# A hybrid S5 and linear-attention layer on one core: operand copies staged through tiles, 16 more weight tiles in the last sweeps, fewer and re-queued conditioning steps

## The chip, the cores and the metric

The kernel runs on one core of a Trainium2 chip, in one launch. The metric is the device time of that launch in microseconds. Before the change three runs took 2925.06, 2934.24 and 2933.97 us, median 2933.97. The names of the engines are those of the profile: PE is TensorE (PEld its weight loads), DVE is VectorE, ACT is ScalarE, POOL is GpSimd and SP is SyncE. SP and POOL issue nearly all transfers, each in the order of its own queue; ACT issues a few.

## The reference

One layer of a decoder. 1088 tokens (64 of the samples, 1024 of the prompt) of width 2048 are normed and modulated by a conditioning vector, then multiplied by one wide matrix whose columns feed two mixers and their gates:

```python
mod = jax.nn.silu(c) @ w_ada + b_ada
shift, scale, gate = jnp.split(mod, 3, axis=-1)
h = rms_norm(x, norm_gain) * (1 + scale[:, None]) + shift[:, None]
u_a, z_a, q, k, v, z_b, g_lr, m_a, m_b = jnp.split(h @ w_in, SPLIT_POINTS, axis=-1)
a_y, sa_re, sa_im = s5_branch(u_a, ...)
a_out = (a_y * jax.nn.silu(z_a)) @ w_a_out
log_a = jax.nn.log_sigmoid((g_lr @ w_gate_up + b_gate).astype(jnp.float32)) / GATE_TAU
b_y, s_gla = gla_branch(q * DK_B ** -0.5, k, v, log_a, s0_gla, gla_norm_gain)
b_out = (b_y.astype(x.dtype) * jax.nn.silu(z_b)) @ w_b_out
merged = jax.nn.sigmoid(m_a) * a_out + jax.nn.sigmoid(m_b) * b_out
y = x + gate[:, None] * (merged @ w_out)
```

All of it is float32. The S5 mixer is a diagonal complex scan in 64 groups; the other mixer is gated linear attention (GLA) with 4 heads. A final norm follows.

## The kernel before

Every wide product is made of three passes: an operand is split into a rounded part (`hi`) and the rest (`lo`), and PE adds hi·hi, hi·lo and lo·hi (`mm3`, lines 71 to 73; in the sweeps lines 1176 to 1178). Weights come in tiles of 128x512 floats (256 KB): SP loads one into a raw tile, ACT makes its `whi`, DVE its `wlo`.

The program has these stages, with their times in the profiled execution:

- 0 to 180 us: `norm_in` loads x and norms it. Then the columns 0 to 2 of `w_in` (the generator `product_k`) are multiplied while the conditioning product runs: 64 loads of 512 KB of `w_ada` (tile `adaraw`, line 195) and 512 small matmuls (`ada_mm`, line 203); each two chunks of it let `modulate` write two of the 16 operands `h[k]` (tiles `hh` and `hl`, lines 266 and 268).
- 180 to 664 us: further columns of `w_in`, with the S5 scan of 16 units woven in.
- 664 to 774 us: columns 20 to 23. Beside them `blocks` writes the right operands of the sweeps to DRAM: the splits of four sums `t1` to `t4` per k through the tile `st` (3 buffers; ACT line 1074, DVE line 1075, POOL's store line 1076, destination `opt`), and three plain quarters `11`, `21`, `22` per k straight from `hh` and `hl` (POOL lines 1079 and 1080, destination `op`, 48 stores in all).
- 774 to 1998 us: the `sweeps`. 48 columns are done by a Winograd scheme of seven half-size products: three groups of eight column pairs, seven sweeps each (`a11`, `a12`, `s1`, `s2`, `s3`, `a22`, `s4`), 384 matmuls of 272 columns a sweep. For each pair `left` loads weights into `raws()` (8 half act tiles and 2 `wraw` tiles, ten in turn); `s1`, `s2`, `s3` and `s4` load two tiles for one and subtract or add them on DVE (line 1109), `s1` and `s2` also store the result to `ws` (lines 1119 and 1122). After a pair, `right` loads the next sweep's operand (line 1142), and the results go to `mas`, `mbs`, `zas`, `zbs` through `fin` or `pt` (line 1196). The GLA mixer (`gla_run`) is woven in: `next(self.steps)` is called at the places in a pair that `self.pace[r]` gives, up to three.
- 1998 to 2500 us: `branch_a` (tile `yt`: 64 loads of 68 KB of the S5 result, line 993, then gelu) and `merge`, which multiplies by `w_a_out` and `w_b_out` in turn, loads `m` (line 1041) for each and stores `mscr`. The conditioning of the output gate (`ada_gates`: 32 loads `gateraw` of 512 KB, line 965, two buffers, and 256 small matmuls) is woven in, one step at the end of each of the three chunks of a product.
- 2500 us to the end: `final`, the product with `w_out` and the last norm.

What stands in the file isn't the order of the queues. Instructions are recorded with the tiles that they read and write, and a scheduler of the language then places them, engine by engine, by its own estimate of when each can start; an instruction recorded late stands early in its queue when its operands and its tiles are there early. A tile with few buffers holds its writers back until a buffer comes free, and a pool opened in the memory of a closed one waits for that one's last reader. Each engine then runs its queue strictly in order. So the 48 stores of lines 1079 and 1080, which need no tile of their own, stand at the head of POOL's queue, and the `yt` loads stand in the third group of the sweeps, when the GLA mixer's memory has come free for them.

Of the kernel before, what the change touches and what calls it, by code (L numbers as in the profile page):

```python
# [10 lines left out]
F32 = mybir.dt.float32  # L11
F32R = mybir.dt.float32r
U8 = mybir.dt.uint8
AF = mybir.ActivationFunctionType
# [4 lines left out]
P = 128  # L19
# [5 lines left out]
T = TS + TP  # L25
CH = [(0, 320), (320, 384), (704, 384)]
HT = T // 2
# [3 lines left out]
QK4 = 512  # L31


class Hybrid:
# [923 lines left out]
    def ada_gates(self):  # L958

        nc, a = self.nc, self.a  # L960
        for j in range(16, 24):
            ps = self.psum(False)
            for k in range(0, KT, 4):
                raw = self.p2.tile([P, 1024], F32, tag="raw", name="gateraw", bufs=2)
                nc.sync.dma_start(raw, a["w_ada"][j][:, k * 256:(k + 4) * 256])
                yield
                self.ada_mm(ps, k, raw, 4)
            yield
            self.ada_out(j, ps)
# [59 lines left out]
    def merge(self, aa):  # L1029

        nc, a = self.nc, self.a
# [3 lines left out]
        def gated(m, keep):  # L1035
# [14 lines left out]
            return ev  # L1050
        ea, eb = gated(self.mas, True), gated(self.mbs, False)
        self.product(a["w_a_out"], range(0, 3), aa, ea)
        bb = [self.branch_b(i) for i in range(8)]
        self.product(a["w_b_out"], range(0, 3), bb, eb)
        for j in range(3, 16):
            self.product(a["w_a_out"], [j], aa, ea)
            self.product(a["w_b_out"], [j], bb, eb)

# [6 lines left out]
    def blocks(self, h):  # L1065

        nc = self.nc
        V = nc.vector
        with ExitStack() as ctx:
            pp = self.pool("blocks", ctx=ctx)  # L1070
# [6 lines left out]
            for k in range(8):  # L1077
                for name, (hi, lo), o in (("11", h[8 + k], 0), ("21", h[k], 0), ("22", h[k], HT)):
                    nc.gpsimd.dma_start(self.opscr[name][k][:, :HT], hi[:, o:o + HT].bitcast(F32))
                    nc.gpsimd.dma_start(self.opscr[name][k][:, HT:], lo[:, o:o + HT].bitcast(F32))  # L1080
                x, y = (pp.tile([P, T], F32, tag=n, name=n, bufs=2) for n in "xy")
# [51 lines left out]
    def sweeps(self, w, groups, h):  # L1133

        nc = self.nc
# [12 lines left out]
        count = [0, 0]  # L1148

        def raws():  # L1150
            i = count[0] % 10
            count[0] += 1
            if i > 7:
                return self.wp.tile([P, QK4], F32, tag="wraw", name="wraw", bufs=2)
            return rawv[i]

        def fin():
            count[1] += 1
            return finv[count[1] % 8]
        n = 0  # L1160
        for g, group in enumerate(groups):
            for r, (an, bn) in enumerate(self.SWEEPS):
                B, N = sets[n % 2], sets[(n + 1) % 2]
                n += 1
                nxt = self.SWEEPS[r + 1][1] if r < 6 else "11" if g + 1 < len(groups) else None
                for i, (pair, dst, silu) in enumerate(group):
                    ps = self.pmm.tile([P, 2, 512], F32, tag="mm2", name="mm", bufs=2)
                    for q in range(2):
                        hi, lo = self.left(w, an, pair, q, self.wscr[i], raws)
                        for k in range(4):  # L1170
                            c = slice(k * P, (k + 1) * P)
                            bhi, blo = B[4 * q + k]
                            for m in range(2):
                                o = ps[:, m, :NC]
# [3 lines left out]
                                nc.tensor.matmul(o, lo[:, c], bh, start=False, stop=q == 1 and k == 3)  # L1178
                            if 4 * q + k in ((), (4,), (2, 6), (1, 4, 6))[self.pace[r]]:
                                next(self.steps, None)  # L1180
# [117 lines left out]
    def run(self):  # L1298
        nc, a = self.nc, self.a
# [59 lines left out]
        self.steps = self.behind()  # L1359
        self.pace = (3, 2, 2, 2, 1, 3, 2)  # L1360
        pairs = lambda j0, d, silu=False: [((j0 + i, j0 + i + 1), (d[i], d[i + 1]), silu) for i in range(0, len(d), 2)]
# [8 lines left out]
        self.steps = self.ada_gates()  # L1370
        self.ticks = ()
        self.merge(aa)
# [79 lines left out]
```

## Time and profile before

| what | value |
|---|---|
| median of three runs | 2933.97 us |
| the profiled execution, its span | 2938.97 us, 2937.2 us |
| PE busy, PEld busy | 96%, 91% |
| DVE, ACT, POOL busy | 58%, 35%, 14% |
| mean granted TensorE clock | 0.982 |
| moved by DMA | 610.52 MB, 208 GB/s over the span |

The page says that PE is the engine that everything waits for. It is read by stretches: in each, the time that PE is not busy, and the time that it runs at half its clock, are what could be saved there; the DMA share (the mean busy share of the 16 DMA engines) and the rows of waits say what it was for. Matmul ends are modelled, so a busy stretch can still hold small waits.

### The profile page before, as it was taken

How to read it: one execution, taken by the hardware profiler on the slowest of the kernel's cores; microseconds unless marked ns; L12 is line 12 of the kernel's file. 1: busy time of each engine (PE TensorE's matmuls, PEld its weight loads, DVE VectorE, ACT ScalarE, POOL GpSimd, SP SyncE). 2: the span in 40 equal slices, each digit the busy share in tenths (PEclk: the TensorE clock that was granted, in tenths of full speed). 3: DMA queues.
4: the chain of work that ended last, by engine and by line, in shares of the span. 5: the costliest groups of instructions: out<-in, count | busy, mean ns of one | idle time of the engine just before them, and what ended most of it. 6: DMA issues, size and time to landing. Idle time of an engine off the chain costs nothing.

```text
span 2937.2 us, 54282 instructions
## 1 busy us (share of the span) xinstructions
PE 2813.0 (96%) x20736; PEld 2669.6 (91%) x20736; DVE 1715.7 (58%) x4016; ACT 1018.9 (35%) x1823; POOL 411.5 (14%) x702
## 2 busy tenths in 40 slices
PE   7999999999899999999999989999999999899987
PEld 4689899999888999998999989999988999899987
DVE  3486777678245786667777535656532322456465
ACT  4222222223233344444344442333221211344434
POOL 1101222121001100011000032011110000203021
PEclk9999999999899999999999999999999999999999
DMA  9944444447668887668867599953575433555455
GB/s 377 386 132 133 117 127 122 114 122 258 235 206 288 295 298 255 187 217 302 292 219 246 194 276 296 319 181 123 173 257 176 136 120 118 184 161 181 145 181 164
DMA packets 321748, 610.52 MB, mean 208 GB/s; under 512 B 47952, under 2 KB 106096, under 8 KB 321360
## 3 DMA queue, kind: packets, MB, share of 16 engines
q1 hardware_dynamic: 256624, 433.51, 46.4%
q0 software_dynamic: 48528, 158.70, 15.6%
q10 hardware_dynamic: 16336, 14.84, 1.5%
q8 instruction: 163, 2.67, 0.4%
q14 instruction: 97, 0.79, 0.1%
HBM read 465.65 MB, written 132.87 MB: 204 GB/s over the span
## 4 chain that ended last, share of the span: by engine, by line
PE 63%; DMA 18%; DVE 8%; issue 7%; ACT 3%; POOL 1%; SPq 1%; DVEq 0%; POOLq 0%; ACTq 0%
PE mm L71 12%; PE mm L72 12%; PE mm L73 12%; PE mm L1178 6%; PE mm L1177 6%; PE mm L1176 6%; DMA raw<-in_w_in_dram 5%; DMA wraw<-in_w_in_dram 2%; DMA hh<-opt 1%; DMA bz<-zbs 1%; DMA raw<-ws 1%; DMA wraw<-in_w_out_dram 1%; PE bg L203 1%; DVE wlo L58 1%; DVE wlo L1130 1%
## 5 line engine op out<-in xcount | busy, mean ns | idle before, releaser
L1176 PE MATMUL mm<-hh,whi 128*128 128x272 f32 x2688 | 788.9, 293 | 25.4 <-ACT whi L1128 13.1
L1178 PE MATMUL mm<-hh,wlo 128*128 128x272 f32 x2688 | 790.2, 294 | 1.6 <-DVE wlo L1130 1.6
L1177 PE MATMUL mm<-hl,whi 128*128 128x272 f32 x2688 | 785.6, 292 | 0.0
L71 PE MATMUL mm<-ahi,whi 128*128 128x384 f32 (+3 forms) x1656 | 547.6, 331 | 17.9 <-DVE y L1248 9.0
L73 PE MATMUL mm<-ahi,wlo 128*128 128x384 f32 (+3 forms) x1656 | 544.2, 329 | 0.6 <-DVE wlo L58 0.4
L72 PE MATMUL mm<-alo,whi 128*128 128x384 f32 (+3 forms) x1656 | 543.5, 328 | 0.0
L1176 PEld LDWEIGHTS mm<-hh,whi 128*128 128x128 f32 x2688 | 514.3, 191 | 31.3 <-ACT whi L1128 14.7
L1178 PEld LDWEIGHTS mm<-hh,wlo 128*128 128x128 f32 x2688 | 513.8, 191 | 5.2 <-DVE wlo L1130 2.4
L1177 PEld LDWEIGHTS mm<-hl,whi 128*128 128x128 f32 x2688 | 514.3, 191 | 3.1 <-issue 1.0
L58 DVE TENSOR_TENSOR wlo<-wraw,whi 128x512 fp32r<-128x512 f32 x368 | 269.5, 740 | 269.8 <-ACT whi L56 268.4
L56 ACT ACTIVATE whi<-wraw 128x512 fp32r<-128x512 f32 x368 | 230.3, 630 | 490.5 <-PE mm L72 278.4
L71 PE MATMUL mm<-hh,whi 128*128 128x384 f32 (+3 forms) x1056 | 344.2, 329 | 9.0 <-ACT hh L266 9.0
L72 PE MATMUL mm<-hl,whi 128*128 128x384 f32 (+3 forms) x1056 | 346.8, 329 | 2.8 <-DVE hl L268 2.8
L73 PE MATMUL mm<-hh,wlo 128*128 128x384 f32 (+2 forms) x1056 | 346.6, 330 | 0.0
L71 PEld LDWEIGHTS mm<-ahi,whi 128*128 128x128 f32 x1656 | 314.6, 190 | 35.2 <-issue 22.8
L73 PEld LDWEIGHTS mm<-ahi,wlo 128*128 128x128 f32 x1656 | 314.5, 190 | 3.9 <-DVE wlo L58 2.5
L72 PEld LDWEIGHTS mm<-alo,whi 128*128 128x128 f32 x1656 | 315.0, 190 | 1.3 <-issue 0.4
L1128 ACT ACTIVATE whi<-raw 128x512 fp32r<-128x512 f32 x270 | 168.6, 628 | 323.3 <-PE mm L1177 191.6
L1130 DVE TENSOR_TENSOR wlo<-raw,whi 128x512 fp32r<-128x512 f32 x270 | 183.9, 684 | 51.4 <-ACT whi L1128 48.6
L71 PEld LDWEIGHTS mm<-hh,whi 128*128 128x128 f32 x1056 | 198.4, 189 | 14.2 <-ACT hh L266 11.5
L72 PEld LDWEIGHTS mm<-hl,whi 128*128 128x128 f32 x1056 | 198.9, 189 | 9.9 <-DVE hl L268 4.7
L73 PEld LDWEIGHTS mm<-hh,wlo 128*128 128x128 f32 x1056 | 198.8, 189 | 3.4 <-issue 2.6
(373 smaller groups left out, 3446.1 us busy)
## 6 DMA issues: line engine op xcount, KB each, us to landing
raw<-in_w_in_dram SPq DMA_DIRECT2D x346, 256.0 KB
wraw<-in_w_out_dram SPq DMA_DIRECT2D x192, 256.0 KB
wraw<-in_w_in_dram SPq DMA_DIRECT2D x182, 256.0 KB
adaraw<-in_w_ada_dram SPq DMA_DIRECT2D x64, 512.0 KB
hl<-opt SPq DMA_DIRECT2D x96, 272.0 KB
hh<-opt SPq DMA_DIRECT2D x96, 272.0 KB
raw<-ws SPq DMA_DIRECT2D x78, 256.0 KB
ws<-raw POOLq DMA_DIRECT2D x77, 256.0 KB, 5.5
```

The source lines that it names most:

```text
L56: nc.scalar.activation(hi, raw, AF.Copy)
L58: nc.vector.tensor_tensor(lo, raw, hi.bitcast(F32), ALU.subtract)
L71: nc.tensor.matmul(ps, hi[:, c], ah[:, sl], start=start, stop=False)
L72: nc.tensor.matmul(ps, hi[:, c], al[:, sl], start=False, stop=False)
L73: nc.tensor.matmul(ps, lo[:, c], ah[:, sl], start=False, stop=stop)
L203: self.nc.tensor.matmul(ps[i:i + 32, :256], self.c32[:, k, :], raw[:, (k - k0) * 256:(k - k0 + 1) * 256], start=k < 4, stop=k >= KT - 4, t ...
L1128: nc.scalar.activation(hi, x, AF.Copy)
L1130: nc.vector.tensor_tensor(lo, x, hi.bitcast(F32), ALU.subtract)
L1176: nc.tensor.matmul(o, hi[:, c], bh, start=q + k == 0, stop=False)
L1177: nc.tensor.matmul(o, hi[:, c], bl, start=False, stop=False)
L1178: nc.tensor.matmul(o, lo[:, c], bh, start=False, stop=q == 1 and k == 3)
```

## The change

Five things are changed.

- `blocks`: the quarters `11`, `21` and `22` are copied by ACT into the same `st` tile (two copies of 128x544 each), and one store of 544 KB takes the place of two of 272 KB. 24 stores and 48 ACT copies stand for 48 stores.
- `pace`: a table for each group in place of one for all; none in the third.
- From the third sweep (`s1`) of the last group to the end of its sixth, the steps of GLA are drained, and a pool `more` in its memory gives 16 further raw tiles, taken in turn with the old ten.
- `ada_gates` loads on POOL's queue in place of SP's.
- In `merge`, from column 3 on, only the products with `w_b_out` call its steps.

```diff
@@ ada_gates
-                nc.sync.dma_start(raw, a["w_ada"][j][:, k * 256:(k + 4) * 256])
+                nc.gpsimd.dma_start(raw, a["w_ada"][j][:, k * 256:(k + 4) * 256])
@@ merge
+        self.ticks = ()
         self.product(a["w_a_out"], range(0, 3), aa, ea)
...
+        gates = self.steps
         for j in range(3, 16):
+            self.steps = iter(())
             self.product(a["w_a_out"], [j], aa, ea)
+            self.steps = gates
             self.product(a["w_b_out"], [j], bb, eb)
@@ blocks
-                for name, (hi, lo), o in (("11", h[8 + k], 0), ("21", h[k], 0), ("22", h[k], HT)):
-                    nc.gpsimd.dma_start(self.opscr[name][k][:, :HT], hi[:, o:o + HT].bitcast(F32))
-                    nc.gpsimd.dma_start(self.opscr[name][k][:, HT:], lo[:, o:o + HT].bitcast(F32))
+                for name, hl, o in (("11", h[8 + k], 0), ("21", h[k], 0), ("22", h[k], HT)):
+                    st = pp.tile([P, T], F32R, tag="st", name="st", bufs=3)
+                    for p in range(2):
+                        nc.scalar.activation(st[:, p * HT:(p + 1) * HT], hl[p][:, o:o + HT].bitcast(F32), AF.Copy)
+                    nc.gpsimd.dma_start(self.opscr[name][k], st.bitcast(F32))
@@ sweeps
         def raws():
-            i = count[0] % 10
             count[0] += 1
+            if sp and count[0] % 2:
+                return sp.tile([P, QK4], F32, tag="raw2", name="raw2", bufs=16)
+            i = (count[0] // 2 if sp else count[0]) % 10
...
+            last = g + 1 == len(groups)
+            pace = ((2, 2, 2, 2, 2, 3, 2), (3, 3, 2, 2, 2, 3, 2), (0,) * 7)[g]
...
+                if last and r == 2:
+                    for _ in self.steps:
+                        pass
+                    sctx = ExitStack()
+                    sp = self.pool("more", ctx=sctx)
+                elif last and r == 6:
+                    sp = None
+                    sctx.close()
...
-                            if 4 * q + k in ((), (4,), (2, 6), (1, 4, 6))[self.pace[r]]:
+                            if 4 * q + k in ((), (4,), (2, 6), (1, 4, 6))[pace[r]]:
@@ run
-        self.pace = (3, 2, 2, 2, 1, 3, 2)
...
-        self.ticks = ()
```

What it moves is seen in the queues. First POOL's queue from its last setting-up instruction on, before (the first of 48 stores; `op_0_254` and the like are DRAM operands, the numbers being those of the tensors):

```order
masks.py:199 AFFINE_SELECT ident<-ident 128x128
L1079 DMA op_0_254<-hh 128x544
L1079 DMA op_1_255<-hh 128x544
L1080 DMA op_0_254<-hl 128x544
L1079 DMA op_0_214<-hh 128x544
L1080 DMA op_1_255<-hl 128x544
L1079 DMA op_1_215<-hh 128x544
```

and the same place now, where the S5 parameters follow at once:

```order
masks.py:199 AFFINE_SELECT ident<-ident 128x128
L415 DMA s5par<-par 128x2368
L421 DMA par<-s5par 128x148
L423 DMA bc<-in_s5bc_dram 128x256
L421 DMA par<-s5par 128x148
```

All 48 stores have left this place. They are now 24 in the stretch of columns 20 to 23, three ahead of each k's four. Its end on POOL's queue, before (`xr` is a tile of the program's last stage whose first three loads stand here; it shares its buffers with `ev`, from which the columns 22 and 23 are stored to `kscr`):

```order
L1076 DMA opt_7_229<-st 128x1088
L1076 DMA opt_7_245<-st 128x1088
L1076 DMA opt_7_237<-st 128x1088
L1076 DMA opt_7_253<-st 128x1088
L1237 DMA xr<-in_xT_dram 128x416 x3
L948 TENSOR_TENSOR on<-on 128x64
```

and now (line 1086 is the new store, line 1080 the old store 1076, line 1257 the old 1237):

```order
L1086 DMA op_7_213<-st 128x1088
L1086 DMA op_7_221<-st 128x1088
L1086 DMA op_7_261<-st 128x1088
L1257 DMA xr<-in_xT_dram 128x416 x3
L1080 DMA opt_7_229<-st 128x1088
L1080 DMA opt_7_245<-st 128x1088
L1080 DMA opt_7_237<-st 128x1088
L1080 DMA opt_7_253<-st 128x1088
L948 TENSOR_TENSOR on<-on 128x64
```

The last four stores now stand behind the three `xr` loads. On PE the first instruction of GLA (line 777) stood before the first matmul of the sweeps:

```order
L71 MATMUL bg<-hh,whi 128x384
L72 MATMUL bg<-hl,whi 128x384
L73 MATMUL bg<-hh,wlo 128x384
L777 MATMUL bg<-gr,wgu 128x64
L1176 MATMUL mm<-hh,whi 128x272
```

and it stands now behind 215 of them:

```order
L1197 MATMUL mm<-hl,whi 128x272
L777 MATMUL bg<-gr,wgu 128x64
L803 MATMUL bg<-q,k 32x32 x2
L1198 MATMUL mm<-hh,wlo 128x272
L1196 MATMUL mm<-hh,whi 128x272
```

The 20 units of GLA end accordingly 0.67 sweeps later, in the middle of the last group's second sweep. Third, POOL's queue at the start of the last group, before (`zas` is a result of the sweeps, `ws` the stored sum of two weight tiles):

```order
L993 DMA yt<-y_106 16x8x136 x4
L993 DMA yt<-y_107 16x8x136 x4
L1196 DMA zas_122<-fin 128x544
L1196 DMA zas_124<-fin 128x544
L993 DMA yt<-y_108 16x8x136 x4
L993 DMA yt<-y_109 16x8x136 x4
L1119 DMA ws_0_262<-raw 128x512
```

and now (lines 1216 and 1125 are the old 1196 and 1119):

```order
L948 TENSOR_TENSOR on<-on 128x256
L1216 DMA zas_126<-fin 128x544
L1216 DMA zas_128<-fin 128x544
L1216 DMA zbs_130<-fin 128x544
L1125 DMA ws_0_262<-raw_20930 128x512
L1125 DMA ws_0_262<-raw_20963 128x512
L1125 DMA ws_0_264<-raw_21000 128x512
L1216 DMA zbs_132<-fin 128x544
```

The `yt` loads are gone from here; they stand in the last group's sixth and seventh sweep. The `gateraw` loads stand on POOL's queue behind the sweeps, between the loads of `m` and the stores of `mscr`, the last behind 2112 of the 5184 matmuls of that part on PE, where it was 1536.

## Rows read from the trace of the kernel before

**Rows 1.** The page: busy time and share of the span by engine.

```profile
PE 2813.0 (96%) x20736; PEld 2669.6 (91%) x20736; DVE 1715.7 (58%) x4016; ACT 1018.9 (35%) x1823; POOL 411.5 (14%) x702
```

**Rows 2.** Stretches: length, busy time of PE, PEld, DVE, ACT, POOL, clock, DMA share, GB/s.

```profile
50.00:150.00 100.00, 91.43 (x684) 64.92 (x681) 41.72 (x105) 20.68 (x31) 20.87 (x39) 0.93 0.99 385
150.00:180.00 30.00, 25.07 (x180) 20.20 (x179) 22.05 (x75) 7.78 (x11) 4.29 (x8) 1.00 0.56 162
...
664.00:748.00 84.00, 84.00 (x507) 84.00 (x506) 70.03 (x94) 32.09 (x54) 16.74 (x32) 1.00 0.74 271
...
774.00:856.00 82.00, 70.10 (x475) 62.72 (x474) 29.82 (x91) 31.20 (x68) 1.95 (x4) 0.83 0.54 168
856.00:1623.00 767.00, 747.48 (x7087) 715.87 (x7086) 533.73 (x1295) 332.39 (x667) 80.58 (x144) 0.99 0.79 262
...
1681.00:1850.00 169.00, 151.73 (x1154) 150.00 (x1153) 79.06 (x123) 56.24 (x70) 47.24 (x88) 0.95 0.93 289
1850.00:1998.00 148.00, 144.27 (x1150) 143.51 (x1149) 96.09 (x143) 58.33 (x79) 21.53 (x39) 1.00 0.71 236
...
2100.00:2300.00 200.00, 194.20 (x1261) 171.31 (x1260) 71.11 (x112) 45.36 (x59) 18.45 (x35) 0.98 0.65 219
```

**Rows 3.** Waits of PE, 34 to 180 us: total, times, longest.

```profile
PE mm L71 <- ACT hh L266: 9.0, 6, 2.7
...
PE bg L203 <- DMA adaraw<-in_w_ada_dram: 1.1, 2, 0.6
```

**Rows 4.** DMA issues: times, KB each, median us to landing.

```profile
opt<-st POOLq DMA_DIRECT2D x32, 544.0 KB, 4.5
...
op<-hl POOLq DMA_DIRECT2D x24, 272.0 KB, 8.9
```

**Rows 5.** Timeline of POOL, lines 1079, 1076, 1237: start, duration, operation, idle before.

```profile
49.27 0.71 POOL L1079 DMA_DIRECT2D op<-hh  x1 [47.96 <-ACT hh L266]
...
673.43 1.11 POOL L1076 DMA_DIRECT2D opt<-st  x2 [28.39 <-DVE st L1075]
...
747.78 0.53 POOL L1076 DMA_DIRECT2D opt<-st  x1 [1.90 <-DVE st L1075]
784.23 0.55 POOL L1237 DMA_DIRECT2D xr<-in_xT_dram  x1 [35.92 <-DMA kscr<-ev]
```

**Rows 6.** The chain that ended last, 0 to 200 us: start, duration.

```profile
94.41 1.98 PE bg L203 x32
```

**Rows 7.** Groups of 664 to 748 us: busy, mean ns, idle before.

```profile
L1076 POOL DMA_DIRECT2D opt<-st x32 | 17.1, 533 | 86.2 <-DVE st L1075 82.6 <-issue 3.7
L1074 ACT ACTIVATE st<-x 128x544 fp32r<-128x544 f32 x24 | 15.7, 658 | 19.1 <-DMA opt<-st 13.6 <-DVE x L1091 3.6 <-DVE y L1084 1.3
```

**Rows 8.** Timeline of ACT: the last thing ahead of GLA's first matmul.

```profile
759.61 0.24 ACT L776 ACTIVATE gr<-gt 96x64 fp32r<-96x64 f32 x1
```

**Rows 9.** Waits of PE and of ACT at the first sweep.

```profile
PE bg L833 <- DVE g L820: 4.9, 2, 4.4
...
ACT ev L637 <- DMA kscr<-ev: 4.8, 3, 3.0
```

**Rows 10.** Waits of PE and DVE, 1681 to 1850 us.

```profile
PE mm L1176 <- ACT whi L1128: 10.5, 2, 5.5
...
DVE raw L1109 <- DMA raw<-in_w_in_dram: 38.4, 12, 8.5
```

**Rows 11.** Loads of `yt`, 1640 to 1860 us, and two stretches of 10 us.

```profile
L993 POOL DMA_DIRECT2D yt<-y x48: 528/530/559, 1683.3 to 1786.4; - x48
...
1700.00:1710.00 10.00, 10.00 (x82) 10.00 (x81) 1.85 (x3) 6.08 (x6) 1.10 (x2) 1.00 0.90 215
1850.00:1860.00 10.00, 10.00 (x83) 10.00 (x82) 4.95 (x8) 3.18 (x4) 0.00 (x0) 1.00 1.04 378
```

**Rows 12.** Waits of SP's queue and of PE, 2095 to 2300 us.

```profile
SPq L965 <- PE bg L203: 119.6, 28, 17.6
...
PE bg L203 <- DMA gateraw<-in_w_ada_dram: 2.9, 2, 2.6
```

More of the change, by code (lines that the diff above doesn't have):

```diff
@@ L1164, in sweeps @@
                 n += 1
+                if last and r == 2:
[4 more added lines that the diff above has]
+                elif last and r == 6:
+                    sp = None
+                    sctx.close()
                 nxt = self.SWEEPS[r + 1][1] if r < 6 else "11" if g + 1 < len(groups) else None
```

## The prediction, written before the changed kernel ran

> **What bounds the kernel now.** I read the busy line first: PE is busy for 2813.0 of 2937.2 us [rows 1], so at most some 124 us of idle time can go, and what its clock fell for. Where these lie is a question for the table of stretches [rows 2]. In each row I count as lost what PE was not busy, and the length times what the granted clock lacks to 1.00:
>
> - 50 to 150 us: 100 − 91.43 = 8.6 idle and 7 for a clock of 0.93; 150 to 180 us: 4.9 idle. Together 20.5. The DMA engines are full here (0.99, 385 GB/s).
> - 774 to 856 us, the first sweep: 11.9 idle and 82 × 0.17 = 13.9 of clock, 25.8 in all.
> - 856 to 1623 us, the next thirteen sweeps: 19.5 and 7.7, spread thinly.
> - 1681 to 1850 us, the last group's start: 17.3 and 8.5, 25.8; the 148 us behind it lose 3.7.
> - 2100 to 2300 us, in `merge`: 5.8 and 4.0.
>
> Third come the waits and time lines of these stretches [rows 3 to 12]. In the first, PE waits 9.0 us for `hh` and 1.1 for `adaraw` [rows 3]. `hh` hangs on the conditioning product, and 32 of its matmuls take 1.98 us [rows 6]: it is the arrival of its 512 KB loads that is slow, and the 48 stores, the first at 49.27 us [rows 5], share the engines with them. In the last group's start DVE waits 38.4 us for weights [rows 10], while 48 of the 64 `yt` loads are issued from 1683.3 to 1786.4 us [rows 11].
>
> **Part 1, the start.** 48 stores of 272 KB [rows 4] are 13.4 MB; at 385 GB/s [rows 2] that is 35 us of full DMA engines, taken out of 50 to 180 us. PE lost only 20.5 us there, so this is the most that can come back; the least is the direct wait for `adaraw`, 1 us. I take the waits behind the loads, 9.0 + 1.1, and 1.9 us of the 7 of clock: **−12** (−20.5 to −1). The rest of the clock I leave, since the operands still come one k at a time.
>
> **Part 2, the blocks and the first sweep.** The stores come back as 24 stores of 544 KB among 32 like them, with 48 ACT copies of the shape of line 1074's, 48 × 658 ns = 31.6 us [rows 7]. ACT was busy for 32.1 of 84 us from 664 to 748 and PE for all 84 [rows 2]: the copies lie beside PE's work, and what counts is when the chain of the tile `st` ends. The 32 stores were issued from 673.43 to 747.78 us [rows 5], 74.35 / 31 = 2.40 us each. At that pace 24 more end 57.6 us later, at 805. By bytes alone, 13.4 MB at the 366 GB/s that 1.00 of DMA share would give (271 / 0.74 [rows 2]), they end 36.5 us later, at 784. Between these, the last four stores are now behind the three `xr` loads, which waited until 784.23 us for the stores to `kscr` [rows 5]: 784 + 4 × 2.40 = 794.
>
> GLA's first matmul needs `gr`, which ACT wrote at 759.61 us [rows 8], 11.8 us behind the last store. It now stands behind 215 matmuls of the first sweep. A matmul of the sweeps without GLA beside it takes 0.129 us (148 us for 1150 [rows 2]), so its place is 774 + 27.6 = 802. `gr` would be ready at 796, 806 or 817 by the three ends. PE then waits for 0, 4 or 15 us; I take 6, near the middle one, which rests on a named wait. What goes is the waiting for GLA at once at the sweep's head: with `gr` and `g` (4.9 us [rows 9]) PE has ACT's wait for `kscr` behind it too (4.8 us [rows 9]), and all of the clock lost there came of such pauses. Of 25.8 I leave 10 (6 idle, 4 of clock): **−16** (−24 with no wait; +4 where the chain ends at 817 and the clock falls as before). ACT now has the first five `whi` of the sweep ahead of the last copies, so PE can start on time.
>
> **Part 3, the last group.** The `yt` loads leave 1683 to 1786 us: they wait for the memory that `more` holds. They are 68 KB each but in small pieces: from 1700 to 1710 us the DMA share was 0.90 at only 215 GB/s, while 1850 to 1860 us had 1.04 at 378 [rows 11]. Without them the weights for `s1` and `s2` come at full rate, and 16 more raw tiles let them come 4 MB ahead. The stall (DVE's 38.4 us for raw tiles, PE's 10.5 for `whi` [rows 10]) is what the 25.8 us stand for. I leave 8 of it, since `s1` and `s2` still load two tiles for one and store the results, and add 5 for the `yt` loads, which return in the sixth and seventh sweep, where 148 us lose just 3.7 today: **−13** (−24 if nothing returns; +5 if the whole of their stall does, beside a wait when the pool's memory is handed back).
>
> **Part 4, conditioning of the gate and `merge`.** SP's queue stood for 119.6 us on PE for buffers of `gateraw`, 28 times [rows 12], and everything behind, the loads of weights, stood with it. On POOL's queue they hold back only loads of `m` and the stores. PE itself waited 2.9 us there for `gateraw` [rows 12], and lost 9.8 us. **−4** (−8 to +6, the upper end where an `m` load is held up behind POOL's head).
> The Trainium skill's page "DMA: Bandwidth & Descriptors" (section "Issuing engines are not separate DMA queues") says that transfers started by any engine share the same 16 DMA engines, and that issuing from another one saves only issue time. By that this term would be 0 and the sum 4 us less. The trace differs in one point: what SP's queue loses here is no issue time but its order behind waits for PE, 119.6 us of them.
>
> **Part 5, GLA and its pace.** The same 20 units at other places: work on PE is conserved, and they end in the middle of the last group's second sweep, ahead of the drain at its third. 0, from −4 to +4 out of the 27 us lost in the middle sweeps [rows 2]. `branch_a` starts with the `yt` loads late: 0, to +10 where the last of them isn't there (they need 103 us for 48 [rows 11], and two sweeps are 98).
>
> **Sum.** −12 − 16 − 13 − 4 = −45. The profiled execution took 2938.97 us, 5 more than the median of 2933.97, so it would take 2894, and the median comes to **2889**. About 0.3%, 8.8 us, is what a measurement of this kernel can tell from no change: faster is below 2925.2, slower above 2942.8.
>
> **The rivals.**
>
> *Slower: the chain of `st` blocks the head of the sweeps.* The 272 KB stores took 8.9 us to land, the 544 KB ones 4.5 [rows 4]. With three buffers a store takes about a third of copy, issue and landing: (2 × 0.66 + 0.53 + 4.5) / 3 = 2.1 us, near the measured 2.40. If landings go to 8.9 us, it is 3.6 us, the last of the 56 is issued at 673 + 55 × 3.6 = 871, and `gr` is ready at 883, 81 us behind its place on PE. At 3.6 us that puts 75 of waiting on the 6 I leave, and the clock falls for 10 more: −45 + 85 = +40, a median of 2974. It decides from about 2.9 us a store on (last store at 833, `gr` at 844, a wait of 43, and again 10 of clock): there the whole gain is gone. For it: ACT already waits 13.6 us for `st` to come free [rows 7], and the loads of the first sweep run beside. Against: the DMA share was 0.74, and 8.9 us was measured where it was 0.99 [rows 2]. Chance 0.12.
> The Trainium skill's page "SBUF — State Buffer" (section "🔬 SBUF: two separate sides", the "DVE blocks DMA" trap) says that a transfer issued by GpSimd starves for descriptors while DVE runs an operation on both port pairs, which speaks for this rival and against gate loads on POOL. The trace disagrees for DVE's work here: with DVE busy for 70 of 84 us, the 32 stores were issued in 533 ns each and landed in 4.5 us.
>
> *No change: the stalls only move.* At the start PE's own work is the bound (−2); the first sweep waits for GLA as long as before, at its new place (−4); the `yt` stall returns whole in the last two sweeps (0). −6, a median of 2928. For it: the bytes are the same, and 1850 to 1860 us, in the sweep ahead of them, had all DMA engines busy already (1.04 [rows 11]). Against: both new places have slack now, the old ones had none. Chance 0.12.
>
> *Less: POOL's queue.* A `gateraw` load that waits for PE holds the `m` loads behind it, which both products of a column need. SP's longest such wait was 17.6 us [rows 12]; if a few such a program come through, `merge` costs 20 instead of −4: −21, a median of 2913. For it: there are two buffers as before, and the last steps now lie later on PE. Against: each `m` load is asked for a column ahead. Chance 0.13.
>
> *More: every lower bound.* −20.5 − 24 − 24 − 8 = −76, a median of 2858. For it: all four are stalls that hang on DMA engines in the wrong stretch. Against: the clock seldom comes back whole. Chance 0.10.
>
> **How the numbers follow.** My forecast has 0.53, with its own range from 2870 to 2910. The range of 2858 to 2932 holds it, the less and the no-change case and half of the more; it leaves out the slower one and some tails, under 0.2. Faster: 0.53 + 0.13 + 0.10 + 0.02 of the no-change case = 0.78; same 0.10; slower 0.12.
>
> **What would show it.** Right: no store in 50 to 150 us, a DMA share there clearly under 0.99 and `hh` waits under 3 us; the last store to `opt` between 784 and 805 us and a first sweep of about 66 us with its clock above 0.9; sweeps three to six of the last group at about 49 us each without `raw` waits on DVE; waits for PE gone from SP's queue in `merge`. Wrong: a start no shorter with the DMA engines free, a long wait of PE for `gr` in the first sweep, the last group's sixth and seventh sweep longer than 55 us, or `m` waited for in `merge`.

## The result, and the profile after

The changed kernel took 2901.05 us (median of 4 runs, 2893.01 to 2903.69) against 2933.04 for the kernel before in the same comparison: ratio 0.9892, 95% interval 0.9865 to 0.9919. A second series on the chip gave 2906.45 us and 0.9909 (0.9887 to 0.9930). So it is 25 to 32 us faster, where 45 were forecast: the time lies inside the forecast's own range of 2870 to 2910 us. The experiments show that this total is right in part by chance: the two terms on the blocks' change, −28 of the −45, come to nothing by themselves (experiment 1); beside them stands a gain by a line that the sum doesn't price (experiment 7), and the last group's gain has a cause that the sum didn't name (experiment 9).

The profiled execution of the changed kernel has a span of 2901.5 us, against 2937.2. By the starts of PE's matmuls (a sweep's length is the distance from its first matmul to the next sweep's first) the 35.7 us come from here:

| stretch | before | after | difference | forecast |
|---|---|---|---|---|
| start to the first sweep | 774.0 | 764.7 | −9.3 | −12 |
| first group (its first sweep) | 431.6 (81.8) | 421.6 (73.0) | −10.0 (−8.8) | −16 |
| second group | 417.7 | 416.8 | −0.9 | 0 |
| last group | 374.8 | 364.9 | −9.9 | −13 |
| behind the sweeps | 939.0 | 933.5 | −5.5 | −4 |

GLA's work that moves from the first group to the last takes its time along, so the groups' differences are not yet gains. And the profiled execution of before is longer than each of the runs beside it, 6 us above their median. How far one profile can stray is seen in experiments 3, 9 and 10, whose instructions stand in the first two groups as in the kernel before: their first sweeps took 76.7, 78.1 and 80.1 us (before 81.8), their first groups 422.9, 424.2 and 431.2 us (before 431.6). So the 10.0 us of the first group are not told from no change by this table.

The table of stretches, after, as in [rows 2] (length, busy time of PE, PEld, DVE, ACT, POOL, clock, DMA share, GB/s): the start, the blocks, and the first sweep in two parts.

```profile
50.00:150.00 100.00, 93.26 (x758) 67.74 (x754) 48.44 (x123) 23.09 (x34) 0.00 (x0) 0.98 0.74 275
150.00:180.00 30.00, 27.61 (x177) 25.22 (x170) 23.66 (x80) 9.29 (x16) 0.00 (x0) 1.00 0.51 136
664.00:748.00 84.00, 84.00 (x509) 84.00 (x508) 52.27 (x70) 42.20 (x74) 19.31 (x37) 1.00 0.87 316
...
764.70:800.00 35.30, 21.43 (x135) 20.75 (x136) 10.86 (x18) 13.94 (x25) 6.96 (x13) 0.79 0.91 332
800.00:837.70 37.70, 37.70 (x292) 35.12 (x291) 16.39 (x51) 15.35 (x34) 0.00 (x0) 0.97 0.65 189
```

The start did what was forecast: POOL issues nothing there, the DMA share falls from 0.99 to 0.74, the loss from 20.5 us to 6.7 + 2 + 2.4 = 11.1. PE's wait for `hh` is halved, from 9.0 us [rows 3]. PE's waits of after from 34 to 180 us (total, times, longest):

```profile
PE mm L71 <- ACT hh L266: 4.5, 4, 1.8
...
PE bg L203 <- DMA adaraw<-in_w_ada_dram: 0.6, 1, 0.6
```

The first sweep did not. It loses 13.9 us of idle time and 7.4 + 1.1 of clock (0.79 in its first half): 22.4, where 10 were forecast and 25.8 lost before. The waits of PE from 764 to 838 us name the place:

```profile
PE mm L1196 <- ACT whi L1134: 13.9, 2, 7.2
PE mm L1196 <- ACT ev L637: 0.5, 1, 0.5
```

Both long waits are for `whi`, none for `gr`. The stores through `st` (count, ns, first and last start) end where the forecast's middle estimate put them, 793.2 us for 794:

```profile
L1080 POOL DMA_DIRECT2D opt<-st x32: 531/531/544, 663.2 to 793.2; - x32
L1086 POOL DMA_DIRECT2D op<-st x24: 531/531/558, 656.3 to 780.3; - x24
```

ACT's time line (start, duration, operation; in brackets its idle time and what ended it) shows what this does to the `whi` of the first sweep, line 1134:

```profile
777.70 0.66 ACT L1085 ACTIVATE st<-hh 128x544 fp32r<-128x544 f32 x1 [1.31 <-issue]
...
779.90 1.13 ACT L1134 ACTIVATE whi<-raw 128x512 fp32r<-128x512 f32 x2
...
784.91 0.66 ACT L1078 ACTIVATE st<-x 128x544 fp32r<-128x544 f32 x1 [1.98 <-DMA op<-st]
...
791.49 0.66 ACT L1078 ACTIVATE st<-y 128x544 fp32r<-128x544 f32 x1 [4.54 <-DMA opt<-st]
795.57 1.15 ACT L1134 ACTIVATE whi<-raw 128x512 fp32r<-128x512 f32 x2 [3.43 <-DMA raw<-in_w_in_dram]
```

SP's loads of the weights in the same stretch (start, length of the group of issues), SP's waits for such loads to land (total, times, longest), and 5 us of the table of stretches:

```profile
766.26 15.93 SPq L1110 DMA_DIRECT2D raw<-in_w_in_dram  x4
783.43 14.45 SPq L1110 DMA_DIRECT2D raw<-in_w_in_dram  x4
SPq L1110 <- DMA raw<-in_w_in_dram: 18.7, 2, 10.9
789.70:794.70 5.00, 0.00 (x0) 0.00 (x0) 0.72 (x1) 0.66 (x1) 0.53 (x1) 0.75 1.03 414
```

PE's two waits of about 7 us have two causes. From 777.70 to the `whi` at 779.90 ACT has no idle time: it makes copies into `st`, while the weights had landed at about 775 (an estimate: SP's shorter wait, 18.7 − 10.9 = 7.8 us, from its issue that ended at 767.3). That is the order of ACT's queue. The next `whi`, 15.7 us later, is another matter. The copies before it wait for buffers, up to 4.54 us, but ACT is through with them at 792.15 and then stands 3.43 us until the weights land; SP waits 10.9 us for the same landing, with the DMA share at 1.03. GLA's `gr` was there at 808.65 us and its first matmul ran at 811.3, so the wait on which the forecast put its price did not occur.

The last group's third to sixth sweeps are nearly free of loss. Its second, third, fourth and seventh sweep in the table of stretches, after:

```profile
1661.13:1716.64 55.51, 54.42 (x502) 53.33 (x501) 38.26 (x85) 28.29 (x51) 8.50 (x15) 1.00 0.70 231
1716.64:1766.39 49.75, 48.39 (x386) 48.01 (x385) 27.71 (x44) 10.55 (x17) 10.79 (x20) 1.00 1.03 398
1766.39:1814.61 48.22, 48.22 (x387) 48.22 (x385) 28.77 (x45) 10.11 (x16) 3.25 (x6) 1.00 1.00 355
...
1911.10:1968.00 56.90, 50.28 (x385) 49.52 (x384) 36.48 (x52) 33.45 (x37) 22.32 (x42) 0.97 0.66 170
```

The loads of `yt` are in its last two sweeps (POOL's issues, after: count, ns, first and last start):

```profile
L993 POOL DMA_DIRECT2D yt<-y x64: 528/530/551, 1893.1 to 1982.0; - x64
```

The sweeps of `s1` and `s2` (third and fourth) run at 398 and 355 GB/s and need 49.75 and 48.22 us, where they took 56.4 and 56.0. The seventh rises from 51.4 to 56.9 us: 5.5 come back, as forecast. But what PE waits for in it is DVE, not a transfer, and DVE's waits for weights in the third to sixth sweep are not gone (PE's longest row of the seventh sweep, DVE's row from 1716 to 1911 us):

```profile
PE mm L1196 <- DVE pt L1207: 6.6, 4, 3.1
DVE raw L1115 <- DMA raw<-in_w_in_dram: 13.6, 6, 4.9
```

The pool `more` moves one thing more than the `yt` loads. The first two `gateraw` loads, which stood in the last group's second sweep, stand in its sixth now, at 1897.8 us, and not behind the sweeps; experiments 8 and 9 turn on this.

In `merge` SP's queue no longer waits for PE; POOL's does, for `gateraw`, 78.9 us in 200 (SP: 119.6 [rows 12]). POOL's waits from 2070 to 2270 us, and PE's for these loads, after:

```profile
POOL gateraw L965 <- PE bg L203: 78.9, 14, 9.6
PE bg L203 <- DMA gateraw<-in_w_ada_dram: 1.5, 1, 1.5
```

### The profile page after: what moved, and what is told of

Same layout as the page of the kernel before. It is cut to its first block, busy times and chain, and to the rows that moved or that the text cites. A ratio compares the mean times of both kernels' runs of the same rounds, so it can differ in the third digit from the quotient of the medians.

```text
span 2901.5 us, 54314 instructions
## 1 busy us (share of the span) xinstructions
PE 2795.2 (96%) x20736; PEld 2660.6 (92%) x20736; DVE 1714.6 (59%) x4016; ACT 1048.4 (36%) x1874; POOL 415.3 (14%) x710
## 4 chain that ended last, share of the span: by engine, by line
PE 64%; DMA 12%; issue 8%; DVE 7%; ACT 2%; POOL 1%; SPq 0%; DVEq 0%; POOLq 0%; ACTq 0%
PE mm L71 11%; PE mm L73 11%; PE mm L72 11%; PE mm L1198 8%; PE mm L1196 8%; PE mm L1197 8%; DMA raw<-in_w_in_dram 4%; DMA wraw<-in_w_out_dram 1%; DMA wraw<-in_w_in_dram 1%; DMA bz<-zbs 1%; DVE wlo L1136 1%; DVE wlo L58 1%; DVE s L295 1%; DMA mx<-mscr 1%; DMA xs<-X 1%
## 5 line engine op out<-in xcount | busy, mean ns | idle before, releaser
L1196 PE MATMUL mm<-hh,whi 128*128 128x272 f32 x2688 | 785.5, 292 | 25.0 <-ACT whi L1134 13.9
L1196 PEld LDWEIGHTS mm<-hh,whi 128*128 128x128 f32 x2688 | 510.5, 190 | 30.7 <-ACT whi L1134 15.7
L71 PE MATMUL mm<-hh,whi 128*128 128x384 f32 (+2 forms) x1056 | 343.7, 329 | 4.9 <-ACT hh L266 4.5
L1134 ACT ACTIVATE whi<-raw 128x512 fp32r<-128x512 f32 x281 | 175.3, 628 | 358.3 <-PE mm L1197 285.6
L1136 DVE TENSOR_TENSOR wlo<-raw,whi 128x512 fp32r<-128x512 f32 x281 | 191.8, 685 | 87.1 <-ACT whi L1134 85.6
```

The source lines that it names most:

```text
L71: nc.tensor.matmul(ps, hi[:, c], ah[:, sl], start=start, stop=False)
L1134: nc.scalar.activation(hi, x, AF.Copy)
L1136: nc.vector.tensor_tensor(lo, x, hi.bitcast(F32), ALU.subtract)
L1196: nc.tensor.matmul(o, hi[:, c], bh, start=q + k == 0, stop=False)
```

## The experiments

Ratios are against the kernel before, with 95% intervals. Shown are the edits to the kernel before, where nothing else is said.

**1. The blocks' change alone.** The hunk `blocks` of the diff, nothing else.

> The kernel before with the change to the blocks alone (quarters copied into st, 24 stores in place of 48). Theory, from the trace of the changed kernel: the start gains 9 us, the first group loses 6 less of idle time and clock, nothing else changes: about 2918 us, ratio 0.995, with PE waiting some 14 us for whi in the first sweep behind the last copies on ACT. By the prediction's own terms (-12 and -16) 2905, ratio 0.990, and no such wait. Rival: the first sweep's loss is only moved, so that only the start counts: 2924, ratio 0.997.

Measured: 2932.61 us, ratio 1.0004 (0.9991 to 1.0018). Nothing. The start gained 10.8 us (the first sweep began at 763.2 us), so the bytes were in the way there. But the first sweep grew from 81.8 to 85.1 us, its first 60 us with a clock of 0.77 (table of stretches of this kernel):

```profile
763.20:823.20 60.00, 39.71 (x252) 36.34 (x252) 20.41 (x57) 24.17 (x50) 6.12 (x12) 0.77 0.75 248
```

PE's two longest waits in the same 60 us, the first again for `whi`:

```profile
PE mm L1178 <- ACT whi L1130: 15.2, 3, 7.9
PE bg L833 <- DVE g L820: 4.7, 1, 4.7
```

The last group, too, was 5.7 us longer. Of the two terms of the forecast that stand on this part (−28) nothing is left; the theory had the wait right and still counted a gain.

**2. The 16 tiles alone**, with the drain of GLA's steps that opens their pool.

> The kernel before with the 16 raw tiles alone (the old table of paces). Theory: the yt loads leave the last group's first sweeps; the last group loses 17 us less, 5.5 of them given back in its seventh sweep already counted: about 2918, ratio 0.995 and the sweeps three to six of the last group 48 to 50 us each. Rival: it is the earlier end of something else (the changed blocks and their bytes) that shortens the last group, and the yt loads cost as much at their new place: 2928 or more, ratio 0.998 to 1.000, the last sweep over 60 us.

Measured: 2909.06 us, 0.9922 (0.9906 to 0.9938), 23 us. The sweeps three to six took 48.6, 48.2, 47.8 and 48.6 us, the seventh 60.2, past the rival's mark of 60. Not expected: the first sweep, more than 800 us earlier, fell from 81.8 to 62.1 us (experiment 7).

**3. The gate's conditioning alone.**

> The kernel before with the change to the gate's conditioning alone (loads on POOL's queue, steps only behind w_b_out from column 3 on). Theory: 4 to 6 us less, about 2929, ratio 0.998, the stretch from the sweeps' end to the last product's start 669 in place of 676 us. Rival: loads of m wait behind gateraw at POOL's head, 2934 or more, ratio 1.000 or above, with waits for m on DVE.

Measured: 2916.58 us, 0.9949 (0.9930 to 0.9967), 15 us, three times what was expected; and in the profile most of it lay in the last group, 360.5 us for 374.8, where no gate step runs.

**4. The changed kernel again**, as the standard for the next two.

> The changed kernel once more, for comparison with the others of this call: ratio 0.989 to the kernel before, about 2901 us.

Measured: 2906.45 us, 0.9909 (0.9887 to 0.9930); first sweep 70.7 us, 12.0 us of waiting for `whi` in it.

**5. Quarters stored in the S5 stretch** (edit to the changed kernel). The quarters go straight from `hh` and `hl` again; a write of 16 columns from an S5 unit's result into the same place must land first.

```diff
@@ s5_unit_b (changed kernel); the quarters' lines of blocks are taken out
+        for i in ((3 * u // 2,) if u % 2 == 0 else (3 * u // 2, 3 * u // 2 + 1)):
...
+            self.bgq.dma_start(d[:, HT - 8:HT + 8], y[:, 0, :16])
+            for p in range(2):
+                nc.gpsimd.dma_start(d[:, p * HT:(p + 1) * HT], hl[p][:, o:o + HT].bitcast(F32))
```

> The changed kernel with the three quarters stored straight from hh and hl by 48 stores again, but each tied to an S5 unit by a small write of 16 columns into its place first, so that they stand between 230 and 640 us, where the DMA share was 0.44. Theory (the chain of st and ACT's order held up the first sweep): PE's 13.9 us of waiting for whi there are gone and the clock is above 0.9, 15 to 20 us less than the changed kernel: about 2883, ratio 0.983. Rival: GLA's first unit, which then stands at the head of the first sweep as it did before the change, breaks up PE's work there as it did then, loss 25 of some 80 us: 2898 to 2903, ratio 0.989.

Measured: 2888.65 us, 0.9858 (0.9838 to 0.9877), 18 us less than the changed kernel in the same series. The stores lie from 262.2 to 655.0 us, the S5 stretch keeps PE busy at a DMA share of 0.51, and the first sweep takes 57.4 us without a wait for `whi`. The S5 stretch before, then the S5 stretch and the first 60 us of that sweep in this kernel's table of stretches:

```profile
180.00:664.00 484.00, 479.55 (x3133) 463.77 (x3133) 364.21 (x1332) 121.80 (x292) 91.90 (x177) 1.00 0.44 121
...
180.00:664.00 484.00, 480.27 (x3131) 466.32 (x3130) 366.78 (x1314) 120.23 (x287) 118.49 (x227) 1.00 0.51 146
...
766.80:826.80 60.00, 60.00 (x463) 56.37 (x464) 24.64 (x65) 26.45 (x54) 1.95 (x4) 0.97 0.68 213
```

The rival falls: GLA's first unit stands at the sweep's head here and breaks nothing up.

**6. Quarters stored late without copies** (edit to the changed kernel): as in 5, but tied to each k of the blocks.

> The changed kernel with the quarters stored straight from hh and hl, tied to each k of the blocks by small writes: the same bytes in the same stretch, but no copies on ACT and 32 in place of 56 stores through st. Theory (chain of st and ACT's order): the waits for whi in the first sweep fall from 13.9 to under 5 us, about 2890, ratio 0.985. Rival (bytes: the weights come late because the DMA engines are full from 748 to 800 us): the waits for whi or raw weights stay at 10 or more, 2898 to 2903, ratio 0.989.

Measured: 2894.29 us, 0.9871 (0.9854 to 0.9889), 12 us less than the changed kernel. The last store to `opt` is issued at 790.4 us, as late as in the changed kernel, and the DMA share in the sweep's first 60 us is 0.83, no lower than the changed kernel's 0.80; but the 48 copies are not in ACT's queue, and the wait is 5.5 us, just over the theory's 5 (PE's waits in those 60 us):

```profile
PE mm L1196 <- ACT whi L1134: 5.5, 2, 4.4
```

So bytes alone are not it: the copies, and the 24 stores through `st` that went with them, cost 8 of the 13.9 us. How much of that is ACT's order and how much the landing of the weights is not separated, since this edit also sends the quarters out earlier, the last of them at 766.3 us.

**7. The drain, without the pool.** The edit holds a second line, which the list of changes ahead of the prediction doesn't name: `raws` counts before it reads the count (`sp` stays `None` here).

```diff
@@ sweeps
         def raws():
-            i = count[0] % 10
             count[0] += 1
...
+            i = (count[0] // 2 if sp else count[0]) % 10
...
+                if last and r == 2:
+                    for _ in self.steps:
+                        pass
```

> The kernel before with one line alone: at the third sweep of the last group the steps of GLA are drained (no pool, no further raw tiles, yt loads where they were). GLA's matmuls stand on PE where the kernel with the 16 tiles has them (second unit 0.71 sweeps behind the first in place of 0.38). Theory (the 20 us that the first sweep lost less there come of this order): first sweep 60 to 66 us, last group as before, about 2917, ratio 0.995. Rival (the first sweep varies between runs, all of the gain is in the last group): first sweep near 80, 2930, ratio 0.999 or above.

Measured: 2923.66 us, 0.9991 (0.9978 to 1.0005). The first sweep took 61.7 us, and on PE GLA's second unit stands 0.71 sweeps behind the first, before 0.38. The drain isn't what moved it. In a program built with the drain and the old count, the instructions of every engine stand as in the kernel before; in one built with the moved count and no drain, they stand as in this experiment (neither was run). So it is the count: each load of the sweeps takes the next one of the ten raw tiles, and the order that the scheduler finds from the first sweep on is another one. The traces show the start of it on SP's queue: four `raw` loads of weights stand ahead of GLA's first load (`maskf`) where two stood. Before, then this kernel:

```profile
729.40 0.37 SPq L1104 DMA_DIRECT2D raw<-in_w_in_dram  x1
731.16 0.45 SPq L1104 DMA_DIRECT2D raw<-in_w_in_dram  x1
751.31 0.33 SPq L690 DMA_DIRECT2D maskf<-in_masks_dram  x1
...
730.68 1.50 SPq L1104 DMA_DIRECT2D raw<-in_w_in_dram  x1
732.82 2.04 SPq L1104 DMA_DIRECT2D raw<-in_w_in_dram  x3
755.40 0.33 SPq L690 DMA_DIRECT2D maskf<-in_masks_dram  x1
```

The moved count is in experiments 2, 7, 8 and 11, where the first sweep takes 61.3 to 62.1 us, and not in 1, 3, 9 and 10, where it takes 76.7 to 85.1; the changed kernel has it too. Some 8 of the 20 us are back in the second sweep (58.2 before, 66.1 here), where GLA's second unit now stands. And the last group rose from 374.8 to 386.2 us, so that the sum is nothing. 48 loads of `yt` now lay 12 us later, against `s1` and `s2`, and the fourth sweep was 64.8 us long, with one wait of PE of 11 us for `whi`; DVE waited there for `ws`, the sums of `s1` written out and read again. That sweep's stretch, this kernel:

```profile
1776.55:1841.32 64.77, 53.53 (x385) 52.74 (x385) 33.01 (x52) 13.73 (x19) 11.82 (x22) 0.88 0.92 298
```

DVE's longest wait in it:

```profile
DVE raw L1109 <- DMA raw<-ws: 21.5, 5, 11.2
```

**8. The pool held, the tiles unused until the sixth sweep**: `if sp and r == 5 and count[0] % 2` in `raws`.

> The kernel before with the pool of 16 tiles as in the second experiment, held from the third sweep of the last group, but used only in its sixth: the yt loads leave the group's first sweeps, the weights come through the old ten tiles. Theory (the yt loads are the stall, as in the prediction): sweeps three to five of the last group 48 to 50 us, 2910, ratio 0.992, as with the tiles. Rival (the tiles matter): sweeps three and four, which load two for one, 52 us or more each, 2916, ratio 0.995.

Measured: 2910.5 us, 0.9941 (0.9926 to 0.9956); sweeps three to six 49.1, 51.0, 48.3 and 48.2 us. The interval overlaps that of experiment 2: the tiles themselves give 3 us in the fourth sweep and no more that can be told; it is the memory they hold. Against experiment 7, which has the same order up to the last group, that is 13 us. But this memory holds back two things, the `yt` loads (from 1894.1 us on) and the first two `gateraw` loads, which are still on SP's queue. The loads of `gateraw` (count, ns, first and last start) before and here:

```profile
L965 SPq DMA_DIRECT2D gateraw<-in_w_ada_dram x32: 327/328/623, 1693.0 to 2279.9; - x32
L965 SPq DMA_DIRECT2D gateraw<-in_w_ada_dram x32: 327/328/424, 1893.8 to 2251.0; - x32
```

So this run doesn't show that the `yt` loads were the stall.

**9. The gate's loads on POOL's queue alone.**

```diff
-                nc.sync.dma_start(raw, a["w_ada"][j][:, k * 256:(k + 4) * 256])
+                nc.gpsimd.dma_start(raw, a["w_ada"][j][:, k * 256:(k + 4) * 256])
```

> The kernel before with the gate's loads on POOL's queue and no other change. Theory (the first two gateraw loads stood on SP's queue among the last group's weights and held those up): last group 361 to 365 in place of 375 us, merge a few us shorter, about 2920, ratio 0.996. Rival (the sparser steps are what helps, in merge): 2930, ratio 0.999.

Measured: 2916.97 us, 0.9965 (0.9951 to 0.9978), 10 us. The last group took 362.7 us for 374.8, and for 373.0 in experiment 10 of the same series, with the `yt` loads where they were, from 1679.1 us on. In the kernel before the first two of these loads stood on SP's queue in the last group's second sweep, among the weights (SP's time line, before):

```profile
1690.39 0.33 SPq L1104 DMA_DIRECT2D raw<-in_w_in_dram  x1
1693.04 1.95 SPq L965 DMA_DIRECT2D gateraw<-in_w_ada_dram  x2
1695.47 2.33 SPq L1104 DMA_DIRECT2D raw<-in_w_in_dram  x3
```

On POOL's queue they are issued 1685.3 and 1686.1 us into the program, in the same sweep: the bytes are the same. SP's own waits at these two loads are only 2.2 and 1.3 us, and behind them many weight loads and a few instructions of the other engines change places too; whether the two loads or the new order makes the 10 us isn't shown. SP's waits at the two loads before (1623 to 1850 us), then PE's here in sweeps two to four, which lose their largest row, the 10.5 us for `whi` of [rows 10]:

```profile
SPq L965 <- DMA raw<-in_w_in_dram: 2.2, 1, 2.2
SPq L965 <- DMA hh<-opt: 1.3, 1, 1.3
...
PE mm L1176 <- DVE pt L1187: 3.6, 2, 3.1
PE mm L1176 <- DVE fin L1187: 3.4, 1, 3.4
PE mm L1176 <- ACT whi L1128: 0.5, 1, 0.5
```

**10. The sparser steps alone.**

> The kernel before with the sparser steps alone, loads on SP's queue. Theory: nothing in the sweeps, up to 6 us in merge, 2927 to 2932, ratio 0.998 to 1.000. Rival: these steps carry the gain of the third experiment, 2917, ratio 0.995.

Measured: 2927.48 us, 1.0002 (0.9990 to 1.0014), and the `whi` waits of the last group stay (11.3 us). The third experiment's gain is the queue's, not the steps'.

**11. Tiles and conditioning without the blocks' change.**

> The changed kernel without its change to the blocks (48 stores at the start as before, old table of paces): the 16 tiles and the gate's conditioning. If the blocks' change is worth nothing, as alone, this is as fast as the changed kernel or faster: 2898 to 2904, ratio 0.989 to 0.991. Rival: beside the other parts the 9 us at the start count in full: 2910, ratio 0.993.

Measured: 2895.28 us, 0.9879 (0.9862 to 0.9897), as fast as the changed kernel or faster: its intervals, 0.9865 to 0.9919 and 0.9887 to 0.9930, reach over this one. The first sweep takes 61.9 us here and 73.0 or 70.7 in the changed kernel. The changed kernel starts its sweeps 9 to 12 us earlier, and by the start of the last group its lead is down to 1 us or so (1603.1 and 1603.8, here 1604.6).

With experiments 3 and 9 this run also says what the `yt` loads are worth once the `gateraw` loads are off SP's queue. The last group takes 360.6 us here, with the `yt` loads late, and 360.5 and 362.7 there, with the `yt` loads in place. Its sweeps three to six gain, 194.7 us for 200.2 and 201.8, and its seventh gives that back, 55.9 for 49.9 and 50.2.

**12. Experiment 5 with the pool closed one sweep earlier**: `elif last and r == 5`.

> The kernel of the fifth experiment (quarters stored in the S5 stretch) with the 16 tiles given back one sweep earlier, at the sixth of the last group, so that the yt loads spread over two sweeps. Theory: the last sweep falls from 55 to 51 or 52 us and the sixth rises by under 2: 2886, ratio 0.984. Rival: the yt loads slow the sixth sweep's weights as they did the second to fourth before: 2890 or more, ratio 0.986.

Measured: 2886.66 us, 0.9857 (0.9834 to 0.9879), not to be told from experiment 5. The `yt` loads spread from 1827.3 to 1935.8 us, the fifth and sixth sweep stay at 47.8 and 48.6, but the seventh is still 55.0 us long: a miss for the theory. Its PE waits are for DVE (`pt`, 4.4 us), not for a transfer. What of `branch_a` on DVE stands before those `pt` was not tried.

Experiments 5 and 12 beat both kernels.

## Why the prediction was right or wrong

- **The start (−12): right**, −9.3 and in experiment 1 −10.8. The bytes left, `hh` waits fell by half, part of the clock came back.
- **The first sweep (−16): wrong.** It said that the last copies matter by way of `gr`, with a price of 6 us, and that PE can start on time since five `whi` stand ahead of the last copies. The last store came when it said (793.2 us), and `gr` cost nothing. But PE waited 13.9 us for later `whi`: once behind copies on ACT, once for weights that landed late beside the moved stores, and the clock fell (0.79 in the sweep's first half). The rival that was written as slower has the chain of `st` at the head of the sweeps, at a smaller price: the stores kept a pace of 2.5 us (656.3 to 793.2 in 55 steps). Experiment 6 takes the copies away and 5 takes the stores away too: 5.5 us and none. GLA's place at the sweep's head, which the forecast made the cause of the loss before, does not decide it: in experiments 5 and 7 GLA's first unit still stands there, and the sweep takes 57.4 and 61.7 us. The 8.8 us that the first sweep of the changed kernel did gain are not this term's, since with the blocks' change alone it takes 85.1 us; they go with the other parts. So parts 1 and 2 together come to 0 alone (experiment 1) and to no gain beside the others (experiment 11), not −28.
- **The last group (−13): the size is near (−9.9), the cause not shown.** The waits were given to the `yt` loads alone. Taking the `gateraw` loads off SP's queue, with `yt` still there (experiment 9), shortens the group by 10 to 12 us, and what the pool does (experiment 8) moves both. In [rows 2] and [rows 11] both lie in the same 20 us, and only `yt` was looked at. With `gateraw` out of the way the late `yt` loads and the 16 tiles give 5 to 7 us and cost 6 in the seventh sweep (experiment 11), so their net worth there is about nothing. That the seventh sweep lost the 5 us put down is luck in part: its waits are for DVE, and with the `yt` loads spread over two sweeps it takes 55.0 us still (experiment 12).
- **Conditioning (−4): right for the stretch named**, 5.5 us less behind the sweeps in the profile. That stretch took 935 to 940 us in the five kernels without this change (before, 1, 2, 7 and 8) and 931 to 932 in 9 and 10; but the total of 10 did not move. Most of the part's gain, 15 us alone, is made in the last group. The loads were listed only where they wait (119.6 us in `merge`), not where the first two of them stand.
- **GLA and its pace (0): a gain was not in the sum.** The table itself does nothing: with the old one the changed kernel's instructions on PE, DVE, ACT and POOL stand in the same order (it was not run). Nor does the drain, added to the kernel before. But the moved count of the raw tiles gives the sweeps another order and takes 20 us from the first (experiment 7), 8 of them back in the second. With both the `yt` and the `gateraw` loads out of the way the last group doesn't lose it again (experiments 2, 8 and 11).
- **The signs.** Of those for being wrong one came in part: the seventh sweep took 56.9 us, over 55, the sixth 48.7. Of those for being right two failed: the first sweep at 66 us with a clock above 0.9 (73.0 us, 0.79 in its first half), and no waits of DVE for raw tiles in the last group's third to sixth sweep (13.6 us).
- **POOL's queue as a rival (−21): did not occur**; POOL waits 78.9 us for PE, and PE waits only 1.5 us for `gateraw` and for no `m`.

Why the next raw tile for each load spreads GLA's units out is open: it lies in the scheduler's estimates, which the traces don't show. Open too is how much of the 20 us comes of GLA's places and how much of the two weight loads that stand earlier.

## What to carry to other kernels

Where stores are moved from one stretch to another, price them at the new place by every queue they enter: here the copies stood ahead of the next stage's weights on ACT, waited up to 4.54 us each for a buffer, and the weights landed late beside the stores. Look for a stretch in which PE is busy and DMA is not (here S5, share 0.44) and tie the stores to it (18 us less in experiment 5). Before a stall is given to the largest transfer beside it, list everything that stands in the queue of the waiting transfer at that time: with two loads for a later stage out of SP's queue the last group was 10 to 12 us shorter. And when an edit is tried in parts, read the parts' diff again: here a line that only moved a count did what the line beside it was credited with, and a pool held back two kinds of loads where one was meant.

## What the runs showed that was not expected

- An edit of experiment 7, by which each load takes the next one of the same ten raw tiles, took 20 us from the first sweep (81.8 to 61.7), put 8 onto the second and 11 onto the last group (374.8 to 386.2), with no change to the total (0.9991).
- With two loads of 512 KB on SP's queue among its weights the last group took 374.8 us, with the same bytes on POOL's queue in the same sweep 362.7, though SP waited only 3.5 us at them. The other 30 loads of that edit lie behind the sweeps.
- With the waits of the first sweep gone its clock came back: 0.77 over its first 60 us in experiment 1, 0.97 in experiment 5.
